# Layer 0's maxima turned two units ahead, lead maxima in written order, and the products of layer 1's modulation dealt anew over three stages

## The chip, the cores and the metric

The kernel runs on one core of a Trainium2 chip. The metric is the device time of one execution in microseconds (us). The engines are TensorE (PE; PEld is its weight load), VectorE (DVE), ScalarE (ACT), GpSimd (POOL) and SyncE (SP), which issues most of the DMAs; ScalarE issues a few as well (ACTq).

## The reference, cut to what matters

Two layers over 1024 latent tokens and 256 context tokens, width 1024, all in 32-bit floats. Layer 0 is grouped-query attention (16 heads, 4 groups of keys and values, head size 64), layer 1 is latent attention (16 heads, keys and values from a compressed 256 columns, queries from 384). Context tokens see only context; latent tokens see both.

```python
def hybrid_layer(x, ctx, c, c_ctx, w_mod, b_mod, norm_w, mixer, mixer_params, cos, sin, with_ctx_out):
    shift, scale, gate = adaln_params(c, w_mod, b_mod)
    shift_c, scale_c, gate_c = adaln_params(c_ctx, w_mod, b_mod)
    h = rms_norm(x, norm_w) * (1.0 + scale[:, None, :]) + shift[:, None, :]
    hc = rms_norm(ctx, norm_w) * (1.0 + scale_c) + shift_c
    y, yc = mixer(h, hc, mixer_params, cos, sin, with_ctx_out)
    x = x + gate[:, None, :] * y
    if with_ctx_out:
        ctx = ctx + gate_c * yc
    return x, ctx
```

`adaln_params` is silu(cond) times a 1024 x 3072 matrix, cut into shift, scale and gate (sections 0, 1 and 2 below). Layer 1 needs shift and scale for both conditions, but its gate only for the latent tokens, at the very end. A mixer projects, normalises queries and keys, rotates them, does softmax attention, multiplies by a silu gate and projects back.

## The kernel before, in words

Every product of 32-bit numbers is made of three products of halves (`mm3`, L105 to L111: high x high, low x high, high x low), with the halves from a cast (L102, L173) and a subtraction (L103, L152). Weights come in pieces of 512 KB through a pool of three buffers, `rawp`, tag `wraw` (`load_weight`, L154): DMA on SP (L169), cast on ACT (L173), subtraction on DVE or POOL (L152). The stages, by the time of the profile:

- Up to about 260 us, a planner (`Plan.at(step, function)`, L276) lays out the projections of layer 0: keys and values, queries, and the first gate tiles. Each tile ends on DVE with L103 to L123 lines; L1123 makes the `t` that TensorE transposes at L1131.
- To 359 us, the rest of the gates of layer 0, in slices of 512 columns by m steps (`gate_slice`, L331; per group c, g an index m from 0 to 3): eight times three products per slice into `mm`, ACT and DVE (L343) behind them. In between, the first two attention units are started (`start_unit`: SP loads KA, KB, QA, QL), and their maxima are computed (the lead).
- To 726 us, attention of layer 0 in 20 units. A unit is a pair of heads with all its queries: 16 latent units, each 10 key tiles, and 4 context units (numbers 4, 9, 18, 19), each two. Score maxima of a later unit (L475, two products side by side on halves of the array, `mx`; reduced on DVE at L484) run between the scores of the present one.
- To 853 us the output projection, to 958 the keys stage of layer 1 (below), to 1100 its queries, to 1140 its gates, to 1560 its attention, then the last projection.

**Turns.** Before a unit's scores, its maxima must lie as rows. `do_shift` (L499) puts a reduction into one of four tiles and leaves a function in `self.turns`: four transposes of 32 x 32 on DVE (L95) into 32 rows of `turned`, and two DMAs of 4 KB on ACT's queue (L510, `shift<-turned`). `run_turns` (L742) runs them between a unit's scores and its product with the values, for the units up to `next_turn` (L760), the next one with any context units right behind it. Each score gets its shift by a product `st<-shift,minus` at L589 over all rows of `shift`. The last latent unit (number 17) is cut into 6 and 4 key tiles, and runs its turns after the 6. `add_up` sums on POOL (L636), `finish` normalises there too (L733), and SP loads and stores around it (L728, L734 and on).

**Modulation of layer 1.** `mod_cols` (L251) makes one block of 128 rows: DVE multiplies 128 x 1024 weights (`wcols`) with a row of the condition and sums along it (L254), once per condition. Section 0 is done in eight blocks of two products by the planner (L1342 and on), sections 1 (two products a block) and 2 (one) by `some_cols` (L1484) in the gate slices. `mod_cols_end` turns the sums and, for section 2, stores them.

**The keys stage.** For each of ten token tiles: `kv_compress` (PE `mm`, 128x288, norm on ACT, DVE L1650 to L1656 and POOL), `kv_latent` (transposes, split), `kv_expand` (products `mmk`, `mmv`; ACT squares, DVE sums `kss` L1704, POOL roots `kn_rs` L135, DVE scales L1687; ACT copies and SP stores v), and `kv_store` (transposes L1723, cast on ACT L1727, subtraction on DVE L1728, four stores on SP). `staged` (L115) overlaps them: a tile is stored one round after it is expanded. DVE keeps the written order there. Then follow the query projections (`proj1`, 128x384) with `wqa`, the four pieces of `l1_w_in` 128x2x384, the first of them ahead of the last tile's store.

## Time and profile before

| | before |
|---|---|
| median of 3 runs (lowest to highest), us | 1649.63 (1649.48 to 1652.47) |
| profiled execution, us | 1649.71 |
| its span, us | 1647.9 |
| granted clock, mean over the span | 0.992 |
| TensorE busy, us | 1603.8 |
| DVE busy, us | 1142.0 |
| POOL busy, us | 957.7 |
| ACT busy, us | 642.2 |

The span is the time between the first and the last instruction that the profile shows. A row of the timeline has the start, the length, the engine, the line, the operation, the tiles out<-in, and in brackets the engine's idle time before it with what ended it. "x2" joins equal neighbours.

### The profile page before, as it was taken

Reading aid. Unit: us, or ns where it says so; the run is one execution under the profiler, and the core shown is the slowest. Engines: PE = TensorE matmul, PEld = TensorE weight load, DVE = VectorE, ACT = ScalarE, POOL = GpSimd, SP = SyncE. Lnnn points to the kernel's source line nnn. Section 1 sums busy time; section 2 is a strip of 40 time slices with the busy share of each in tenths; the row PEclk is TensorE's granted clock in tenths of the full one; section 3 lists DMA queues with packets and bytes.
Section 4 is the critical chain, followed back from the end, with each engine's and each line's share of the span. In section 5 each row is a group of like instructions: output and inputs, shape, how many; then the busy total and the mean of one; then the engine's idle time right before and its main releaser. Section 6 shows DMA issues by size and latency. Waiting matters only on the chain.

```text
span 1647.9 us, 26555 instructions
## 1 busy us (share of the span) xinstructions
PE 1603.8 (97%) x9836; PEld 1181.2 (72%) x9836; DVE 1142.0 (69%) x1939; ACT 642.2 (39%) x943; POOL 957.7 (58%) x628
## 2 busy tenths in 40 slices
PE   8999899999999999989999999999999999999998
PEld 5776788775555555557887899887766767767587
DVE  3765986678898888716566667765788788788231
ACT  4643221125554655422234543341534444435310
POOL 2773540118899899933334555450768778777521
PEclk9999999999999999999999999999999999999999
DMA  9545667851444332257324776777566565563451
GB/s 320 178 137 180 186 186 234 247 144 46 107 96 107 97 98 78 59 145 223 119 77 131 214 234 174 221 204 196 127 150 143 136 136 121 136 144 76 124 182 66
DMA packets 215358, 246.26 MB, mean 149 GB/s; under 512 B 19962, under 2 KB 157426, under 8 KB 215228
## 3 DMA queue, kind: packets, MB, share of 16 engines
q1 hardware_dynamic: 214260, 244.31, 53.3%
q8 instruction: 78, 1.28, 0.3%
q14 instruction: 52, 0.43, 0.1%
q10 hardware_dynamic: 968, 0.25, 0.1%
HBM read 170.71 MB, written 73.63 MB: 148 GB/s over the span
## 4 chain that ended last, share of the span: by engine, by line
PE 81%; DVE 6%; DMA 5%; POOL 4%; issue 2%; ACT 1%; SPq 1%; ACTq 0%; DVEq 0%; POOLq 0%
PE st L589 19%; PE av L650 8%; PE mm L109 7%; PE avt L650 7%; PE mm L110 7%; PE mm L111 7%; PE mx L441 4%; PE y L109 3%; PE y L111 3%; PE y L110 3%; PE mx L475 2%; DVE wb L152 1%; POOL acp L636 1%; PE mx L451 1%; DVE t L1123 1%
## 5 line engine op out<-in xcount | busy, mean ns | idle before, releaser
L636 POOL TENSOR_TENSOR acp<-acp,p 128x1024 f32<-128x1024 f32 x188 | 448.8, 2387 | 12.6
L596 ACT ACTIVATE p<-st 128x1024 f32<-128x1024 f32 x328 | 336.4, 1027 | 165.0 <-PE st L589 156.4
L443 DVE TENSOR_REDUCE m<-mx 128x1 f32<-128x512 f32 x256 | 175.6, 691 | 65.3 <-PE mx L441 59.4
L636 POOL TENSOR_TENSOR acp<-p 128x1024 f32<-128x1024 f32 x34 | 81.5, 2398 | 201.3 <-ACT p L596 201.2
L484 DVE TENSOR_REDUCE m<-mx 128x1 f32<-128x1024 f32 x128 | 150.8, 1220 | 45.6 <-PE mx L475 44.7
L650 PE MATMUL avt<-p,v 128*64 128x512 f32 x672 | 149.4, 596 | 0.0
L650 PE MATMUL av<-p,v 128*64 128x512 f32 x640 | 141.1, 595 | 0.0
L152 POOL TENSOR_TENSOR wb<-wraw,wa 128x512 fp32r<-128x512 f32 (+3 forms) x65 | 91.1, 1415 | 77.3 <-ACT wa L173 77.2
L109 PE MATMUL mm<-wa,hh 128*128 128x512 f32 (+2 forms) x336 | 125.5, 373 | 2.0 <-ACT hh L1023 2.0
L589 PE MATMUL st<-QH,KH 64*128 64x512 f32 x320 | 122.7, 407 | 0.1
L111 PE MATMUL mm<-wa,hl 128*128 128x512 f32 (+2 forms) x336 | 120.9, 360 | 1.4 <-DVE hl L1026 1.4
L110 PE MATMUL mm<-wb,hh 128*128 128x512 f32 (+2 forms) x336 | 120.6, 359 | 0.0
L589 PE MATMUL st<-QH,KL 64*128 64x512 f32 x320 | 118.1, 391 | 0.0
L589 PE MATMUL st<-QL,KH 64*128 64x512 f32 x320 | 117.7, 390 | 0.0
L109 PE MATMUL y<-wa,oh 128*128 128x512 f32 (+1 forms) x296 | 114.1, 386 | 2.0 <-DVE yt L880 1.4
L111 PE MATMUL y<-wa,ol 128*128 128x512 f32 (+1 forms) x296 | 113.5, 384 | 0.6 <-DVE ol L863 0.6
L110 PE MATMUL y<-wb,oh 128*128 128x512 f32 (+1 forms) x296 | 113.5, 383 | 0.0
L650 PEld LDWEIGHTS avt<-p,v 128*64 128x64 f32 x672 | 46.3, 137 | 93.2 <-issue 85.0
L650 PEld LDWEIGHTS av<-p,v 128*64 128x64 f32 x640 | 44.4, 137 | 87.9 <-issue 87.3
L109 PE MATMUL mm<-hh,wa 128*128 128x512 f32 (+1 forms) x264 | 104.0, 394 | 0.0
L110 PE MATMUL mm<-hl,wa 128*128 128x512 f32 (+1 forms) x264 | 102.5, 388 | 0.0
L111 PE MATMUL mm<-hh,wb 128*128 128x512 f32 (+1 forms) x264 | 102.1, 387 | 0.0
(259 smaller groups left out, 4026.7 us busy)
## 6 DMA issues: line engine op xcount, KB each, us to landing
wraw<-in_l_w_in SPq DMA_DIRECT2D x28, 512.0 KB
wcols<-in_l_w_mod_t SPq DMA_DIRECT2D x24, 512.0 KB
KH<-k1h SPq DMA_DIRECT2D x32, 320.0 KB
KL<-k1l SPq DMA_DIRECT2D x32, 320.0 KB
rb<-rrow SPq DMA_DIRECT2D x72, 128.0 KB
mraw<-in_l_w_mod SPq DMA_DIRECT2D x16, 512.0 KB
wraw<-in_l_w_out SPq DMA_DIRECT2D x16, 512.0 KB
QA<-q0h SPq DMA_DIRECT2D x32, 256.0 KB
```

Source lines behind the costliest of these rows:

```text
L109: pe.matmul(ps, lhsT=lh(k), rhs=rh(k), start=first and i == 0, stop=False)
L110: pe.matmul(ps, lhsT=lh(k), rhs=rl(k), start=False, stop=False)
L111: pe.matmul(ps, lhsT=ll(k), rhs=rh(k), start=False, stop=last and i == len(ks) - 1)
L152: eng.tensor_sub(lo, a, b)
L441: pe.matmul(held["m"][:, cs], lhsT=q[:, t * P:(t + 1) * P], rhs=k[:, ks], start=j == 0, stop=j == len(pairs) - 1)
L443: dve.reduce_max(s["m"][:, i, n:n + 1], held["m"], axis=AX.X)
L475: pe.matmul(m[:, n * 512:n * 512 + 512], lhsT=q[:, i * P:(i + 1) * P], rhs=k[:, n * 512:n * 512 + 512], start=True, stop=True)
L484: dve.reduce_max(s["m"][:, i, 0:1], m, axis=AX.X)
L589: pe.matmul(ps[:, n * 512:(n + 1) * 512], lhsT=lh, rhs=rh, start=j == 0, stop=j == last)
L596: act.activation(p, ps, AF.Exp, scale=self.ops["scale"])
L636: pool.tensor_add(t, a, b)
L650: pe.matmul(s["av"][64 * n:64 * n + 64, :], lhsT=s["v"][:, kt, u["vc"]:u["vc"] + 64], rhs=p[:, n * 512:(n + 1) * 512], start=kt == kts[0], ...
```

## The change

- **Turns.** `next_turn` now also goes over context units that follow the next unit, so a context unit is turned two units ahead of itself, and `turned` has three places (rows 0, 32 and 96) by turns.
- **Lead.** The gate slices of group 1 from (m = 0, column 512) on are written out in fixed order on TensorE, and two pairs of maxima at a time stand behind slices (1, 1024) to (3, 512), with one group of them in the middle of (3, 0). Both lead units are started together.
- **Loads of a new group of keys.** KA, then QA and QL, then KB.
- **Modulation.** Section 0: five blocks by the planner, ten single products at steps 107.2 to 133 where eight pairs stood at steps 82.2 to 131.2. The gate slices get the three blocks left of section 0 and section 1 (22 products for 24). Section 2 goes to the keys stage of layer 1: one product behind `kv_store` of tiles 0 to 7, from weights in `rawp` (tag `wraw`), written in place.

Where rows move. On TensorE in the lead, before (mm are gate products, mx the maxima of a lead unit):

```order
L111 MATMUL mm_3178<-hh_130,wb_2371 128x512
L475 MATMUL mx_3046<-KA_2960,QA_2966 128x512 x2
L109 MATMUL mm_3178<-hh_130,wa_2370 128x512
L110 MATMUL mm_3178<-hl_131,wa_2370 128x512
L111 MATMUL mm_3178<-hh_130,wb_2371 128x512
L475 MATMUL mx_3079<-KA_2960,QA_2966 128x512 x2
```

After:

```order
L109 MATMUL mm_3050<-hhc_748,wa_2352 128x256
L110 MATMUL mm_3050<-hlc_749,wa_2352 128x256
L111 MATMUL mm_3050<-hhc_748,wb_2353 128x256
L475 MATMUL mx_3079<-KA_2897,QA_2901 128x512 x2
L475 MATMUL mx_3083<-KA_2897,QA_2901 128x512 x2
L109 MATMUL mm_3087<-hh_130,wa_2352 128x512
```

Behind three gate products stood one pair of maxima, and so on; now two pairs of maxima stand together behind a whole slice.

On ScalarE near the end of layer 0's attention, before (p are the exponentials of unit 16's last tile and unit 17's first six, the DMAs its turns):

```order
L596 ACTIVATE p_6627<-st_6784 128x1024
L510 DMA shift_2954<-turned_89 1x4x128 x2
L671 COPY os_6840<-avt_6801 128x512
L596 ACTIVATE p_6844<-st_6853 128x1024
L596 ACTIVATE p_6844<-st_6863 128x1024
L596 ACTIVATE p_6845<-st_6875 128x1024
L596 ACTIVATE p_6845<-st_6886 128x1024
L596 ACTIVATE p_6846<-st_6899 128x1024
L596 ACTIVATE p_6846<-st_6910 128x1024
L510 DMA shift_2954<-turned_89 1x4x128 x4
L596 ACTIVATE p_6956<-st_6960 128x1024
```

After:

```order
L596 ACTIVATE p_6602<-st_6759 128x1024
L510 DMA shift_2891<-turned_89 1x4x128 x6
L671 COPY os_6827<-avt_6776 128x512
L596 ACTIVATE p_6831<-st_6840 128x1024
L596 ACTIVATE p_6831<-st_6850 128x1024
L596 ACTIVATE p_6832<-st_6862 128x1024
L596 ACTIVATE p_6832<-st_6873 128x1024
L596 ACTIVATE p_6833<-st_6886 128x1024
L596 ACTIVATE p_6833<-st_6897 128x1024
L596 ACTIVATE p_6931<-st_6935 128x1024
```

The four copies for the units 18 and 19 moved from behind unit 17's first six tiles to the turn of unit 16, where two stood.

On DVE at the end of the keys stage, before (from tile 7's store on; kss to kn belong to tile 9):

```order
L1728 SCALAR_TENSOR_TENSOR tl_9427<-tp_9421,w_kn_7173,th_9426 128x512
L1728 SCALAR_TENSOR_TENSOR tl_9438<-tp_9432,w_kn_7173,th_9437 128x512
L1704 TENSOR_REDUCE kss_9459<-sq_9457 128x8
L133 TENSOR_SCALAR kn_ms_9461<-kss_9459 128x8
L1704 TENSOR_REDUCE kss_9485<-sq_9483 128x8
L133 TENSOR_SCALAR kn_ms_9487<-kss_9485 128x8
L1687 TENSOR_TENSOR kn_9468<-mmk_9443,kn_rs_9463 128x512
L1687 TENSOR_TENSOR kn_9495<-mmk_9469,kn_rs_9489 128x512
L1728 SCALAR_TENSOR_TENSOR tl_9503<-tp_9497,w_kn_7173,th_9502 128x512
L1728 SCALAR_TENSOR_TENSOR tl_9514<-tp_9508,w_kn_7173,th_9513 128x512
```

After:

```order
L1737 SCALAR_TENSOR_TENSOR tl_9439<-tp_9433,w_kn_7148,th_9438 128x512
L254 SCALAR_TENSOR_TENSOR wcols_9444,cols2_71<-wcols_9444,u0_8249 128x1024
L152 TENSOR_TENSOR wb_9531<-wraw_9538,wa_9530 128x384
L260 TENSOR_TENSOR top3_84<-cols2_71,colsT_112 128x8
L95 STREAM_TRANSPOSE turned_89<-top3_84 32x32 x4
L1713 TENSOR_REDUCE kss_9469<-sq_9467 128x8
L152 TENSOR_TENSOR wb_9531<-wraw_9544,wa_9530 128x384
L133 TENSOR_SCALAR kn_ms_9471<-kss_9469 128x8
L1713 TENSOR_REDUCE kss_9495<-sq_9493 128x8
L133 TENSOR_SCALAR kn_ms_9497<-kss_9495 128x8
L1696 TENSOR_TENSOR kn_9478<-mmk_9453,kn_rs_9473 128x512
L1696 TENSOR_TENSOR kn_9505<-mmk_9479,kn_rs_9499 128x512
```

Between the store and the next tile's sums stand the modulation product of block 7, its end, and two halves of the query weights' subtractions (L152), which before stood some tiles ahead. (Lines after the first edits count higher in the changed kernel: its L1737 is L1728 of before.)

The diff:

```diff
--- before.py
+++ after.py
@@ -248,9 +248,9 @@
                 dve.tensor_tensor(s1, tv, bias, op=ALU.add)
                 dve.scalar_tensor_tensor(A[l][:, ks, :], s1, 1.0, nw, op0=ALU.add, op1=ALU.mult)
 
-    def mod_cols(w, u, junk, sec, k, conds=2):
-
-        for j in range(conds):
+    def mod_cols(w, u, junk, sec, k, conds):
+
+        for j in conds:
             dve.scalar_tensor_tensor(junk, w, 0.5, u[:, j, :], op0=ALU.mult, op1=ALU.mult, accum_out=sums_of[sec][:, k, j:j + 1])
 
     def mod_cols_end(sec):
@@ -503,7 +503,7 @@
             dve.reduce_max(m[:, :8], s["m"], axis=AX.X)
 
             def turn():
-                at_ = 32 * (self.units.index(u) % 2)
+                at_ = (0, 32, 96)[self.units.index(u) % 3]
                 r = turned[at_:at_ + 32, :]
                 turn_squares(r, raw(m))
                 for n in range(2):
@@ -759,6 +759,8 @@
                     cut = 6 if u is self.last_lat else 0
                     next_turn = t + 1
                     while next_turn + 1 < len(self.units) and len(self.units[next_turn]["kts"]) <= 4:
+                        next_turn += 1
+                    while next_turn + 1 < len(self.units) and len(self.units[next_turn + 1]["kts"]) <= 4:
                         next_turn += 1
                     if not WIDE[self.l]:
                         next_turn = None
@@ -1339,8 +1341,8 @@
         sp.dma_start(w, ins["l1_w_mod_t"][sec * D + k * P:sec * D + (k + 1) * P, :])
         gate_in[k] = w
 
-    def cols_mult(sec, k):
-        mod_cols(gate_in.pop(k), gate_in["u"], small.tile([P, D], BF16, name="junk", tag="junk", bufs=1), sec, k)
+    def cols_mult(sec, k, j):
+        mod_cols(gate_in[k], gate_in["u"], small.tile([P, D], BF16, name="junk", tag="junk", bufs=1), sec, k, (j,))
 
     plan.at(46, more_room)
     at_step = 47.6
@@ -1356,10 +1358,10 @@
     plan.at(67.8, cols_room)
     for j in range(2):
         plan.at(72.5 + 4 * j, cond_rows, j)
-    for k in range(KT):
-        plan.at(77 + 7 * k, cols_fetch, 0, k)
-        plan.at(82.2 + 7 * k, cols_mult, 0, k)
-    plan.at(138, mod_cols_end, 0)
+    for k, steps in enumerate(((107.2, 111.2), (115.2, 119.2), (121.5, 124), (126.5, 128.5), (131, 133))):
+        plan.at(steps[0] - 6, cols_fetch, 0, k)
+        for j in range(2):
+            plan.at(steps[j], cols_mult, 0, k, j)
     weight("g1", 2048, 120, (120.2, 122.2, 124.2, 127.2), (125.2, 127.1, 129.2, 132.2))
     for m in range(2):
         for s0 in range(0, NT, 512):
@@ -1409,22 +1411,27 @@
         g = u["g"]
         r = slice(64 * (g % 2), 64 * (g % 2) + 64)
         lat = u["kind"] == "lat"
+        new = False
         if g not in at.kcache:
             KA = kp.tile([P, NT], F32R, name="KA", tag="KA")
             KB = kp.tile([P if HALVES[0] else 65, NT], F32R, name="KB", tag="KB")
             if HALVES[0]:
-                for t, src in ((KA, k0h), (KB, k0l)):
-                    for n in range(2):
-                        sp.dma_start(raw(t[64 * n:64 * n + 64, :]), src[g // 2, r, :])
+                for n in range(2):
+                    sp.dma_start(raw(KA[64 * n:64 * n + 64, :]), k0h[g // 2, r, :])
             else:
                 sp.dma_start(raw(KA[0:64, :]), k0h[g // 2, r, :])
                 sp.dma_start(raw(KA[64:128, :]), k0l[g // 2, r, :])
                 sp.dma_start(raw(KB[0:64, :]), k0h[g // 2, r, :])
                 pool.memset(raw(KB[64:65, :]), -1.0)
+            new = True
             at.kcache[g] = dict(KA=KA, KB=KB)
         KA, KB = at.kcache[g]["KA"], at.kcache[g]["KB"]
         if HALVES[0]:
-            return l0_load_halves(u, at, lat, KA, KB)
+            s = l0_load_halves(u, at, lat, KA, KB)
+            if new:
+                for n in range(2):
+                    sp.dma_start(raw(KB[64 * n:64 * n + 64, :]), k0l[g // 2, r, :])
+            return s
         qp = at.qp if at.started % 4 < 3 else at.qp2
         QA = qp.tile([P, NL], F32R, name="QA", tag="QA")
         QB = qp.tile([65, NL], F32R, name="QB", tag="QB")
@@ -1479,15 +1486,15 @@
     for j in range(2):
         sp.dma_start(u[:, j, :], ud[j:j + 1, :].broadcast_to([P, D]))
     junk = mw.tile([P, D], BF16, name="junk", tag="junk", bufs=1)
-    blocks = [(sec, k) for sec in (1, 2) for k in range(KT)]
+    blocks = [(0, k) for k in range(5, KT)] + [(1, k) for k in range(KT)]
 
     def some_cols(n):
 
-        for _ in range(n):
+        for _ in range(min(n, len(blocks))):
             sec, k = blocks.pop(0)
             w = mw.tile([P, D], F32, name="wcols", tag="wcols")
             sp.dma_start(w, ins["l1_w_mod_t"][sec * D + k * P:sec * D + (k + 1) * P, :])
-            mod_cols(w, u, junk, sec, k, 3 - sec)
+            mod_cols(w, u, junk, sec, k, range(2))
             if k == KT - 1:
                 mod_cols_end(sec)
 
@@ -1499,20 +1506,22 @@
     pieces = []
     wo = [load_weight(ins["l0_w_out"], KT, 0, 512, 2, todo=pieces)]
     with tc.tile_pool(name="wkg0b", bufs=2, **right) as wkg:
-        for s0 in (0, 512):
-            gate_slice(0, 1, 0, s0, 512, ws["g1"], hT, ps_mm, wkg)
-            some_cols(2)
-            at.step += 1
-        pieces.pop(0)()()
+        gate_slice(0, 1, 0, 0, 512, ws["g1"], hT, ps_mm, wkg)
+        at.step += 1
     stG.close()
     at.open_early(stE)
-    at.start_unit()
-    with tc.tile_pool(name="wkg0b", bufs=2, **right) as wkg:
+    for _ in range(2):
+        at.start_unit()
+
+    def two_maxima():
+        at.maxima(at.done + 2, 2)
+
+    with tc.tile_pool(name="wkg0b", bufs=2, **right) as wkg, tc.manual_schedule(engines={mybir.EngineType.PE}):
         for m in range(4):
-            for s0 in range(0, NT, 512) if m else (1024,):
-                gate_slice(0, 1, m, s0, min(512, NT - s0), ws["g1"], hT, ps_mm, wkg)
-                if (m, s0) != (3, 1024):
-                    at.maxima(min(at.done + 2, 14), 2)
+            for s0 in range(0, NT, 512) if m else (512, 1024):
+                gate_slice(0, 1, m, s0, min(512, NT - s0), ws["g1"], hT, ps_mm, wkg, {KT // 2: two_maxima} if (m, s0) == (3, 0) else {})
+                if (m, s0) >= (1, 1024) and (m, s0) != (3, 1024):
+                    two_maxima()
                 at.step += 1
                 at.run_turns()
                 if s0 == 512:
@@ -1731,8 +1740,20 @@
 
         kept = []
 
+        u = st.enter_context(tc.tile_pool(name="urow1", bufs=1, **right)).tile([P, D], F32, name="u0", tag="u0")
+        sp.dma_start(u, ud[0:1, :].broadcast_to([P, D]))
+
+        def gate_cols(k):
+            w = rawp.tile([P, D], F32, name="wcols", tag="wraw")
+            sp.dma_start(w, ins["l1_w_mod_t"][2 * D + k * P:2 * D + (k + 1) * P, :])
+            mod_cols(w, u.unsqueeze(1), w, 2, k, (0,))
+            if k == KT - 1:
+                mod_cols_end(2)
+
         def store_all_but_last(tt, held):
             kept.append(held) if tt == TT - 1 else kv_store(tt, held)
+            if tt < KT:
+                gate_cols(tt)
 
         with in_order(mybir.EngineType.DVE):
             staged(range(TT), kv_compress, kv_latent, later, later, kv_expand, store_all_but_last)
```

## The prediction

> **What bounds the kernel now.** I read the page first, then the windows for the granted clock, then the waits of TensorE in the timeline, and last the rows of the engines that end those waits. Two lines of the page:
>
> ```profile
> span 1647.9 us, 26555 instructions
> PE 1603.8 (97%) x9836; PEld 1181.2 (72%) x9836; DVE 1142.0 (69%) x1939; ACT 642.2 (39%) x943; POOL 957.7 (58%) x628
> ```
>
> TensorE is busy for 1603.8 of 1647.9 us. The number of its products isn't changed, so this change can win only at the 44 us in which it idles, at the time in which it runs at half clock, and at pairs of products that follow each other badly. The windows show the clock (columns: window, length, busy time of PE, PEld, DVE, ACT, POOL, then the granted clock, the DMA share and GB/s):
>
> ```profile
> 200.00:210.00 10.00, 7.75 (x33) 6.49 (x33) 9.66 (x13) 2.22 (x4) 6.15 (x4) 0.83 0.58 176
> 320.00:330.00 10.00, 8.10 (x21) 4.99 (x21) 2.02 (x2) 0.98 (x2) 0.00 (x0) 0.66 1.04 249
> 530.00:540.00 10.00, 7.55 (x34) 3.68 (x32) 4.64 (x3) 2.11 (x3) 7.35 (x4) 0.83 0.51 129
> 700.00:720.00 20.00, 14.86 (x104) 8.33 (x102) 3.00 (x4) 6.51 (x7) 8.78 (x6) 0.83 0.50 136
> ```
>
> A clock of 0.83 over 10 us is 3.4 us at half clock, of which half, 1.7 us, is lost; 0.66 over 10 us and 0.83 over 20 us are 6.8 us, 3.4 lost. Each of these windows holds one wait of TensorE (start, length, instruction, in brackets the idle time before it and what ended it):
>
> ```profile
> 187.64 0.66 PE L1131 MATMUL tp<-ident,t 128*128 128x128 f32 x4 [1.83 <-DVE t L1123]
> 202.25 1.08 PE L1131 MATMUL tp<-ident,t 128*128 128x128 f32 x4 [2.29 <-DVE t L1123]
> 321.90 1.19 PE L475 MATMUL mx<-KA,QA 64*128 64x512 f32 x2 [2.83 <-issue]
> 536.56 0.76 PE L589 MATMUL st<-shift,minus 64*128 64x512 f32 x1 [2.16 <-DMA shift<-turned]
> 706.89 0.79 PE L589 MATMUL st<-shift,minus 64*128 64x512 f32 x1 [5.14 <-DMA shift<-turned]
> ```
>
> So a wait of 2.16 to 5.14 us is followed by 3.4 or 6.8 us at half clock, and the one of 1.83 is not. The change touches the causes of all five waits. [...]
>
> **Projections.** DVE has eight pairs of modulation products in this stage, ahead of L1123, whose result TensorE's transposes wait for:
>
> ```profile
> 181.85 1.22 DVE L254 SCALAR_TENSOR_TENSOR junk<-wcols,urow 128x1024 bf16<-128x1024 f32 x1
> ...
> 183.11 2.19 DVE L254 SCALAR_TENSOR_TENSOR junk<-wcols,urow 128x1024 bf16<-128x1024 f32 x1
> ...
> 185.23 1.75 DVE L152 TENSOR_TENSOR wb<-wraw,wa 128x512 fp32r<-128x512 f32 x1
> ...
> 194.87 1.22 DVE L254 SCALAR_TENSOR_TENSOR junk<-wcols,urow 128x1024 bf16<-128x1024 f32 x1
> ```
>
> The pair at 181.85 takes 1.22 + 2.19 = 3.4 us of the chain before the wait of 1.83; the pair that ends with 194.87 takes 2.4 before the wait of 2.29. Both pairs leave these places: more goes than was waited for, so both waits go, with the clock after the second: 1.83 + 2.29 + 1.7 = 5.8. Ten single products come back, in later tiles and each behind L1123. There one delays the next tile's chain by 1.22, and the L152 of 1.75 still stands in the chain of the four tiles that load gate weights; I leave 0.8 for what stays. Taken: **-5.0**, bounds -3.0 and -5.8.
>
> **Gate slices.** DVE does 22 products here instead of 24 and TensorE waits nowhere between 288 and 319 us, so nothing is to be had; the cover is TensorE's own products. What counts is that DVE's last one comes earlier, because the loads of the lead units start behind it.
>
> **Lead.** First the ends of the m steps of group 1's gates (m = 1, 2, and the end of m = 3), with two of the maxima between them, then the loads on SP, and of DVE's products the one that is the last in the new order (two follow it now):
>
> ```profile
> 302.38 0.40 PE L109 MATMUL mm<-hh,wa 128*128 128x512 f32 x1
> ...
> 316.15 0.40 PE L109 MATMUL mm<-hh,wa 128*128 128x512 f32 x1
> ...
> 329.87 0.50 PE L475 MATMUL mx<-KA,QA 64*128 64x512 f32 x2
> ...
> 331.19 0.49 PE L475 MATMUL mx<-KA,QA 64*128 64x512 f32 x2
> ...
> 359.08 0.50 PE L475 MATMUL mx<-KA,QA 64*128 64x512 f32 x2
> ```
>
> ```profile
> 312.17 1.16 SPq L1418 DMA_DIRECT2D KA<-k0h  x2
> ...
> 315.93 0.60 SPq L1395 DMA_DIRECT2D QA<-q0h  x1
> ```
>
> ```profile
> 305.82 1.23 DVE L254 SCALAR_TENSOR_TENSOR junk<-wcols,urow 128x1024 bf16<-128x1024 f32 x1
> ```
>
> A bare m step takes 316.15 - 302.38 = 13.77 us, for 60 products of 512 columns (0.23 each). Steps 2 and 3 take 359.08 - 316.15 = 42.93, that is 15.4 more than two bare ones: 2.83 of wait, 3.4 of half clock, and 9.2 for 14 pairs of maxima. A pair itself takes 0.23 (3.2 in all), and the period 329.87 to 331.19, three products and one pair, is 1.32 instead of 4 x 0.23 = 0.91: 0.4 us for going over from one kind to the other and back, 14 times, the other 5.9. After the change the same pairs stand in seven groups: 7 x 0.4 = 2.9, so 3.0 go. The loads start when DVE's last product has left their room, and now begin with KA, go on with QA, and leave KB to the last. The product at 305.82 ends at 307.1, so KA is issued between 307.1 and 308.5 (a small store that stood ahead of it is gone) and no longer at 312.17. From KA's issue to the first maxima took 321.90 - 312.17 = 9.7; the two KB loads that stood in between (655 KB at the 249 GB/s of that window) are 2.6 of it. That gives 314.2 to 315.6, ahead of 316.15, where the first maxima now stand. So wait and half clock go as well: 2.83 + 3.4 + 3.0 = 9.2, taken as **-9.0** for small waits on the two score buffers; bounds -6.5 (2 us of wait, half a window of low clock less) and -9.8.
>
> **Turns.** The copies of the turned maxima into the shift rows, issued on ScalarE's queue (length from first issue to last), and first products behind a turn:
>
> ```profile
> 504.05 4.55 ACTq L510 DMA_DIRECT2D shift<-turned  x2
> 525.10 7.53 ACTq L510 DMA_DIRECT2D shift<-turned  x4
> ...
> 681.39 1.23 ACTq L510 DMA_DIRECT2D shift<-turned  x2
> 695.43 9.09 ACTq L510 DMA_DIRECT2D shift<-turned  x4
> ```
>
> ```profile
> 511.98 0.40 PE L589 MATMUL st<-QA,KA 64*128 64x512 f32 x2
> ...
> 689.23 0.40 PE L589 MATMUL st<-shift,minus 64*128 64x512 f32 x2
> ```
>
> At the end of the stage the four copies of 695.43 are issued by 704.5 and land 2.4 us later, at 706.89: 5.14 of wait and 3.4 of half clock. Now all six belong to the turn of 681.39. At that turn's rate (1.23 for two) they take 3.7, are issued by 685.1 and land 2.4 to 3.9 later, by 689.0; the first product that reads them ran at 689.23 without a wait. So **-8.5**, bounds -8.5 and +2.3 (at the rate of the 7.53 row six take 11.3, land at 696.6, and 7.4 of wait and 3.4 of clock come back).
>
> At unit 9's start 2.16 + 1.7 = 3.9 go, since two copies remain there and not four. But the four now stand one unit earlier, at 504.05, where the queue was slow too. In the 7.53 row the last copy, held back on a semaphore that a load of SP used before it, landed 3.9 after the last issue. Moved there, four are issued between 509.8 (4.55 + 1.2) and 511.6 (7.53) and land by 511.8 to 515.5, against products that read them from 512.7 on: 0 to 2.8 of wait, up to 1.7 of clock. Taken: **-2.5**, bounds -3.9 and +0.6.
>
> **Keys.** Eight products move to the keys stage of layer 1, with nine loads of 512 KB through the three slots that the next weights use. The rows: a wait of DVE in a long tile and the splits of two short ones, the key transposes of two short tiles and the query projection on TensorE, and what a piece of weights takes from issue over cast to split:
>
> ```profile
> 896.17 0.69 DVE L1704 TENSOR_REDUCE kss<-sq 128x8 f32<-128x512 f32 x1 [1.12 <-ACT sq L1702]
> ...
> 944.60 1.40 DVE L1728 SCALAR_TENSOR_TENSOR tl<-tp,w_kn,th 128x512 fp32r<-128x512 f32 x2
> ...
> 950.82 1.40 DVE L1728 SCALAR_TENSOR_TENSOR tl<-tp,w_kn,th 128x512 fp32r<-128x512 f32 x2
> ```
>
> ```profile
> 946.33 1.03 PE L1723 MATMUL tp<-ident,kn 128*128 128x128 f32 x8
> ...
> 952.67 1.03 PE L1723 MATMUL tp<-ident,kn 128*128 128x128 f32 x8
> 953.46 0.42 PE L109 MATMUL mm<-wa,hh 128*128 128x384 f32 x1
> ...
> 957.73 1.03 PE L1723 MATMUL tp<-ident,kn 128*128 128x128 f32 x8
> ```
>
> ```profile
> 924.84 0.37 SPq L169 DMA_DIRECT2D wraw<-in_l_w_in  x1
> ```
>
> ```profile
> 928.26 0.51 ACT L173 CAST wa<-wraw 128x384 fp32r<-128x384 f32 x1 [1.46 <-DMA wraw<-in_l_w_in]
> ```
>
> ```profile
> 925.98 1.04 POOL L152 TENSOR_TENSOR wb<-wraw,wa 128x384 fp32r<-128x384 f32 x1 [0.33 <-ACT wa L173]
> ```
>
> The first products of the stage stand in long tiles, where one wait of DVE for ScalarE (1.12) already covers nearly all of 1.22; they hide. In the last tiles DVE goes round in 950.82 - 944.60 = 6.22 us against TensorE's 952.67 - 946.33 = 6.34: a product of 1.22 there makes DVE the slower one, and what covers it is only that the splits of the query weights (the row of 925.98 is one) leave the tiles before. Three such products come ahead of the split of 950.82, 3.7 us less the slack of about 2.2 that I give DVE for those splits and for 0.1 a tile: it moves to 952.3, and the last product ends at 952.3 + 1.4 + 1.2 = 954.9. Before, the four pieces of the query weights were loaded by 925. Now each takes its slot from a product: the third is issued behind the last product. Loaded and cast as in the rows (928.26 - 924.84 = 3.4) and split (0.5 + 1.04) it is there at 959.8; TensorE wants it in the middle of 953.46 to 957.73. The fourth is issued behind a store that waits on ScalarE behind the third's cast, about 959.8, is cast from 963.2, and half of it is split by DVE behind the next tile's L1728, by about 965.7. TensorE wants it at 956.7: 9.0 late, the third's wait within it. Two waits of over 2.16 give at least one stretch at half clock, 1.7. Taken: **+10.7**; bounds +4 (no lag on DVE, pieces landing in 2 us) and +15 (6.8 us more at half clock, and slower loads).
>
> **How the numbers follow.** -5.0 - 9.0 - 8.5 - 2.5 + 10.7 = -14.3. The profiled execution took 1649.71, the median is 1649.63; 1649.7 - 14.3 = **1635.4 us**. What a measurement here can tell from no change is 0.2%, 3.3 us.
>
> The rivals:
> - **The weights are not late.** If the third and fourth piece come through before 956, the four gains stand alone: 1649.7 - 25.0 = 1624.7. For it: a piece needs only 3.4 us from issue to cast. Against: the slot of the third is held until the last product. 0.16.
> - **DVE becomes the bound of the keys stage, and the kernel is slower.** If none of the eight products is hidden and each is stretched as in the row of 183.11, they cost 8 x 2.19 = 17.5; with 9.0 and 3.4 for the late weights 29.9, so 1649.7 - 25.0 + 29.9 = 1654.6. It decides from 28.3 us in this stage on. Against: in the long tiles DVE has waits that take a product in. 0.06.
> - **The lead doesn't get its loads earlier.** If KA and QA come 3 us later than I put them, 2.83 and 3.4 stay: 1641.6. For it: the margin above is 0.5 to 2 us; against: what holds their issue back, DVE's products, is cut. 0.14.
> - **The wait moves with the copies.** If six copies go at the slow rate, 10.8 comes back at unit 17: 1646.2. For it: 9.09 for four; against: 1.23 for two at that very turn. 0.10.
> [...]
>
> The forecast keeps 0.50; its own bounds are about 1629 to 1642. The range 1624 to 1646 takes in the first, third and last rival and nearly all of the fourth. Faster by over 0.2%: 0.88; within: 0.05; slower: 0.07 (the second rival and a little of the fourth with late weights).
>
> **What would show it.** In the profile after: no waits of over 1 us at L1131 between 180 and 225; the gate steps m = 2 and 3 in about 34 us without a low clock; no wait near 703, perhaps one of 1 to 3 us near 512; and a wait of TensorE of 7 to 10 us in two parts at the first 128x384 products of layer 1, with a low clock there. The prediction is wrong if that last wait is missing or twice as long, or if copies at 681 take over 8 us.

## The result, and the profile after

| | before | after |
|---|---|---|
| median, us (runs beside each other) | 1649.48 (7) | 1638.80 (7) |
| lowest to highest, us | 1645.92 to 1653.03 | 1636.82 to 1642.93 |
| profiled execution, us | 1649.71 | 1642.93 |
| granted clock, mean over the span | 0.992 | 0.996 |

The ratio is 0.9937, with a 95% interval of 0.9923 to 0.9951, that is 10.4 us less (8.1 to 12.7). The execution that was profiled after the change happens to be the longest of its seven, so its trace shows only 6.8 of it. From its page, the busy time of each engine:

```profile
PE 1599.2 (97%) x9836; PEld 1185.3 (72%) x9836; DVE 1143.3 (70%) x1939; ACT 640.8 (39%) x943; POOL 958.7 (58%) x628
```

The number of products is the same. I cut both traces at the same instructions of TensorE (their starts in the timelines) and compare stage by stage:

| from, to | before | after | change | predicted |
|---|---|---|---|---|
| start to the transposes of the fifth tile, 78.00 / 81.82 | 78.00 | 81.82 | +3.8 | 0 |
| to the first gate product of group 1, 288.60 / 285.92 | 210.60 | 204.10 | -6.5 | -5.0 |
| to the first scores, 359.42 / 347.64 (the lead) | 70.82 | 61.72 | -9.1 | -9.0 |
| to the scores behind the waits of units 8 and 9, 564.63 / 548.79 | 205.21 | 201.15 | -4.1 | -2.5 |
| to the output projection, 727.68 / 705.13 | 163.05 | 156.34 | -6.7 | -8.5 |
| to the first key transposes of layer 1, 886.78 / 867.05 | 159.10 | 161.92 | +2.8 | 0 |
| to the last transposes of `qan` of the first queries, 1007.11 / 999.46 | 120.33 | 132.41 | +12.1 | +10.7 |
| to the last product, 1643.18 / 1636.36 | 636.07 | 636.90 | +0.8 | 0 |

The five stages that the change touches give -14.3 together, as forecast; the three that it doesn't touch give +7.4. Two of these vary from run to run by themselves: the same transposes began at 78.98 and 79.14 in the profiles of the first and the ninth experiment below, in which nothing before it differs from the changed kernel; and the wait for `yt` at the head of the output projection, 1.43 in the trace of before and 3.74 in that of after, was between 1.11 and 3.75 in the eleven experiments, near 1.1 to 1.7 in seven of them and 2.6 to 3.8 in four. So most of this belongs to the run and not to the change. Not all of the start can be settled: in the one profile of before the transposes of the fifth tile began at 78.00, ahead of all twelve profiles of the changed kernel and the experiments (78.59 to 81.93). The stages that the change touches repeat better. Over the profiles of experiments that leave them alone, the projections took 204.03 to 204.15, the lead 61.72 to 61.73 and the keys stage 132.21 to 132.94; the attention of layer 0 took 356.80 to 357.49, but 358.79 in the sixth experiment and 360.15 in the tenth.

**Clock.** The windows of after that answer to those of before:

```profile
200.00:210.00 10.00, 10.00 (x48) 7.98 (x48) 9.93 (x15) 3.41 (x6) 7.14 (x6) 1.00 0.35 108
320.00:330.00 10.00, 10.00 (x57) 7.90 (x57) 6.93 (x8) 2.18 (x4) 0.00 (x0) 1.00 0.73 204
530.00:540.00 10.00, 10.00 (x92) 7.06 (x90) 9.89 (x13) 8.22 (x8) 9.69 (x6) 1.00 0.73 169
700.00:720.00 20.00, 19.43 (x113) 13.72 (x110) 4.43 (x6) 4.08 (x5) 7.14 (x5) 1.00 0.57 161
940.00:945.00 5.00, 0.90 (x4) 0.30 (x2) 3.04 (x7) 0.45 (x2) 3.24 (x2) 0.79 0.77 219
945.00:950.00 5.00, 4.81 (x17) 4.21 (x18) 2.19 (x5) 1.25 (x4) 1.00 (x1) 0.53 0.73 195
```

All four low windows of before are at 1.00; a new one stands at 940 to 950, in the keys stage. One more, 0.66 over 730 to 735, lies behind the wait for `yt` of 3.74, in a stage that the change leaves alone.

**TensorE's waits**, at the places of the five of before, and then in the keys stage:

```profile
189.49 0.60 PE L1133 MATMUL tp<-ident,t 128*128 128x128 f32 x4
...
201.48 0.63 PE L1133 MATMUL tp<-ident,t 128*128 128x128 f32 x4
...
313.57 0.73 PE L475 MATMUL mx<-KA,QA 64*128 64x512 f32 x4
...
501.19 0.47 PE L589 MATMUL st<-shift,minus 64*128 64x512 f32 x1 [0.97 <-DMA shift<-turned]
...
685.57 0.40 PE L589 MATMUL st<-shift,minus 64*128 64x512 f32 x2
...
933.00 0.50 PE L109 MATMUL mmk<-wa,kvh 128*128 128x512 f32 x1 [1.06 <-DVE kn L1696]
...
941.05 0.44 PE L110 MATMUL mm<-wb,hh 128*128 128x384 f32 x1 [0.76 <-DVE wb L152]
...
945.11 1.01 PE L109 MATMUL mm<-wa,hh 128*128 128x384 f32 x2 [3.45 <-ACT wa L173]
...
960.65 0.52 PE L1882 MATMUL tp<-ident,qan 128*128 128x128 f32 x3 [1.23 <-DVE qan L1875]
```

The two at the transposes, the one at the first maxima and the one of the last unit are gone, the one of 2.16 has become one of 0.97 a unit earlier. What came is 0.49, 0.44 and 1.06 for `kn` in three short tiles, 0.76 and 3.45 for weights, and 1.23 for `qan`.

**The lead and the turns**, on SP's and ScalarE's queues, and the DVE product that ends last before the loads:

```profile
304.38 1.15 SPq L1420 DMA_DIRECT2D KA<-k0h  x2
...
306.86 0.60 SPq L1397 DMA_DIRECT2D QA<-q0h  x1
```

```profile
303.12 1.23 DVE L254 SCALAR_TENSOR_TENSOR junk<-wcols,urow 128x1024 bf16<-128x1024 f32 x1
```

```profile
491.54 6.47 ACTq L510 DMA_DIRECT2D shift<-turned  x4
...
665.60 3.91 ACTq L510 DMA_DIRECT2D shift<-turned  x6
```

The product ends at 304.35 and KA is issued at 304.38. The six copies at 665.60 took 3.91 (I had put 3.7), the four at 491.54 took 6.47.

### The profile page after: what moved, and what is told of

It reads as the page before. It is cut to its first block, busy times and chain, and to the rows that moved or that the text cites. A ratio compares the mean times of both kernels' runs of the same rounds, so it can differ in the third digit from the quotient of the medians.

```text
span 1641.1 us, 26569 instructions
## 1 busy us (share of the span) xinstructions
PE 1599.2 (97%) x9836; PEld 1185.3 (72%) x9836; DVE 1143.3 (70%) x1939; ACT 640.8 (39%) x943; POOL 958.7 (58%) x628
## 4 chain that ended last, share of the span: by engine, by line
PE 82%; DMA 5%; POOL 4%; DVE 4%; issue 3%; ACT 1%; SPq 1%; ACTq 0%; DVEq 0%; POOLq 0%
PE st L589 20%; PE av L650 9%; PE mm L109 8%; PE avt L650 8%; PE mm L111 8%; PE mm L110 7%; PE mx L441 4%; PE y L109 4%; PE y L110 4%; PE y L111 4%; PE mx L475 2%; DVE wb L152 1%; PE mx L451 1%; PE tp L1133 1%; PE pm L216 1%
## 5 line engine op out<-in xcount | busy, mean ns | idle before, releaser
L152 POOL TENSOR_TENSOR wb<-wraw,wa 128x512 fp32r<-128x512 f32 (+3 forms) x65 | 91.9, 1427 | 78.1 <-ACT wa L173 78.1
```

Of the source, the lines that this page charges most:

```text
L152: eng.tensor_sub(lo, a, b)
```

## The experiments

Each is one edit of the changed kernel. Time differences are taken from ratios to before, measured beside it. An interval is some 0.15 to 0.2% on either side, 3 us, so where less matters I go by the traces, cut as in the table.

**1. Turns undone.** Context units are turned one unit ahead again, with two places.

```diff
-                at_ = (0, 32, 96)[self.units.index(u) % 3]
+                at_ = 32 * (self.units.index(u) % 2)
...
-                    while next_turn + 1 < len(self.units) and len(self.units[next_turn + 1]["kts"]) <= 4:
-                        next_turn += 1
```

> The changed kernel with the turns as before (each context unit turned by the unit right ahead of its neighbours, two places in turned). The traces put 4.1 us at units 8 and 9 and 6.7 us at unit 17 on the turns. Theory: part of that is given back at once in the output projection, where TensorE now waits 3.74 us for yt (1.43 before) since the last units' stores are not earlier; with the old turns that wait falls back to about 1.5, and the kernel is some 8 us slower than the changed one. Rival: the longer wait in the output projection has nothing to do with the turns; it stays at 3.7 and the kernel is some 10.8 us slower. Second rival: the six copies at one turn cost something too, and the kernel is less than 6 us slower.

1646.32 us, ratio 0.9976 (0.9965 to 0.9988): 6.4 us more than the changed kernel. From the first scores to the output projection it took 366.85, against 357.49 changed and 368.26 before. The four copies stand behind the six tiles again, and so does the wait:

```profile
678.62 9.05 ACTq L510 DMA_DIRECT2D shift<-turned  x4
```

```profile
689.91 0.79 PE L589 MATMUL st<-shift,minus 64*128 64x512 f32 x1 [4.97 <-DMA shift<-turned]
```

The four take 9.05, as in before (9.09), so the length goes with four copies at that place. In the trace the turns are worth 9.4 of the 10.8 that attention gained. The wait for `yt` was short here, 1.11; but it is as short in experiments that keep the turns (1.31 in the second), so the gain isn't given back there, and that theory falls. The times alone don't separate the 6.4 from the theory's 8 or from the second rival's 6: the two intervals are about 2 us on either side.

**2. Narrow products in the keys stage.** Each of the eight products takes 32 of its 1024 columns and leaves out the rest of its sum; the loads stay.

```diff
-            mod_cols(w, u.unsqueeze(1), w, 2, k, (0,))
+            mod_cols(w[:, :32], u[:, :32].unsqueeze(1), w[:, :32], 2, k, (0,))
```

> The changed kernel with the eight products of the keys stage cut to 32 of their 1024 columns (the sums of section 2 leave out the rest); loads, slots, the end of the section and its store stay. Theory: the length of the products on DVE makes DVE the slower engine in the short tiles (3.2 us by the trace) and pushes the last product, the end of the section and with it the fourth piece's load back; about 5 us faster than the changed kernel, with a wait of about 1 to 3 us left for the fourth piece. Rival: the late weights are set by slots and queues alone; only the 3.2 go. Second rival: the products are the whole cost; 12 us faster, no wait left at the first 128x384 products.

1633.34 us, ratio 0.9901 (0.9883 to 0.992): 6 us less than the changed kernel. The keys stage took 127.96, 7.6 above before and 4.5 below the changed kernel. TensorE's two longest waits up to the last `qan` now:

```profile
929.38 0.45 PE L109 MATMUL mm<-wa,hh 128*128 128x384 f32 x1 [1.84 <-ACT v L1718]
...
947.34 0.52 PE L1882 MATMUL tp<-ident,qan 128*128 128x128 f32 x3 [1.62 <-DVE qan L1875]
```

The waits for `kn` in the short tiles are gone with the multiplication. But 7.6 of the 12.1 stay though DVE multiplies next to nothing: the larger part of the price doesn't come from the products' length. What remains in this run are the loads in the three slots and the section's end. By the trace the weights are in it: ScalarE waits 4.42 for a piece (its cast is at 927.01), and the copy of `v` behind that cast is what the wait of 1.84 is for. No run takes the loads away and keeps the products, so the share of each is not shown.

**3. Products early.** Two products a tile in tiles 0 to 3, none after.

```diff
-            if tt < KT:
-                gate_cols(tt)
+            if tt < KT // 2:
+                gate_cols(2 * tt)
+                gate_cols(2 * tt + 1)
```

> The changed kernel with two products a tile behind the stores of tiles 0 to 3, none behind 4 to 7. Theory: the products in the short tiles and the late slots are the cost, and the long tiles have room for most of two products (DVE waits 0.56 and 1.12 us for ScalarE in them, against 2.44): no wait for query weights, no DVE wait in the short tiles, 9 to 12 us faster than the changed kernel. Rival: the nine loads and the DMA traffic are the cost wherever they stand; within 3 us of the changed kernel.

1635.98 us, ratio 0.991 (0.9893 to 0.9927): 4.4 less, not the 9 to 12 expected. The query weights are in time, but the long tiles take one product and not two:

```profile
908.86 0.47 PE L109 MATMUL mmv<-wa,kvh 128*128 128x512 f32 x1 [3.54 <-DVE kvn L1665]
```

The second product of a tile is late by 0.85 at 884.23 and by 0.84 at 895.20, and behind the last, where TensorE waits 3.54, comes the section's end as well.

**4. The section's end late.** `mod_cols_end(2)` (a sum, four transposes, the store `gated<-turned`) moves behind the last tile's store.

```diff
-            if k == KT - 1:
-                mod_cols_end(2)
...
             kv_store(TT - 1, kept[0])
+            mod_cols_end(2)
```

> The changed kernel with the end of section 2 (its addition, four transposes on DVE and its small store on SP) put behind the last tile's store, out of the way of the query weights. Theory: the small store stands ahead of the fourth piece's load on SP and holds it about 3 us (939.84 against the last product's end at 937.5); without it the piece is issued 2 to 3 us earlier and the kernel is 2 to 4 us faster than the changed one. Rival: the slot that the last product holds, or the store of v ahead of the load, sets the issue; no difference beyond 1 us.

1638.58 us, ratio 0.9926 (0.9909 to 0.9944): 1.8 less, within the noise. The trace tells more. In the changed kernel SP's queue read:

```profile
929.69 1.55 SPq L169 DMA_DIRECT2D wraw<-in_l_w_in  x2
...
939.84 0.29 SPq L263 DMA_DIRECT2D gated<-turned  x1
940.23 0.37 SPq L1719 DMA_DIRECT2D vd<-v  x1
940.65 0.45 SPq L169 DMA_DIRECT2D wraw<-in_l_w_in  x1
```

With the store out of the way the fourth piece follows a store of v at 931.57, 2.9 earlier when both are counted from the first tile's key transposes, and the wait for it is 2.34 in place of 3.45:

```profile
936.89 0.44 PE L109 MATMUL mm<-wa,hh 128*128 128x384 f32 x1 [2.34 <-ACT wa L173]
```

Between the last two key transposes that is 2.3 less, and 1.5 of it is lost again by the last `qan`. So the store does hold the fourth piece back, and mending that alone is worth little.

**5. Section 2 in the attention of layer 1.** The eight products move out of the keys stage, one to a unit, with the row of the condition in a slot of `rawp`.

```diff
+                        if end and self.l == 1:
+                            if cols:
+                                cols()
+                            cols = more.pop(0)() if more else None
...
+            held_u["u"] = rawp.tile([P, D], F32, name="u0", tag="wraw")
...
+    more = [lambda: None] * 5 + [lambda k=k: gate_cols(k) for k in range(KT)]
+    at.run(24, 2, pieces, lambda: first.extend(fetch_first(1, 3)), more)
```

> The changed kernel with the eight products of section 2 taken out of the keys stage and put into layer 1's attention, one behind the turn of each of units 6 to 13, its weights loaded a unit ahead through the same three slots (the condition's row holds one of them). Theory: the keys stage is as before again (12 us less by the trace), and DVE has room in a unit of 25.3 us in which it is busy for 20.3, so the kernel is 8 to 12 us faster than the changed one, with TensorE without waits in layer 1's attention. Rival: next to POOL the products take 2.2 and delay the maxima that TensorE waits for, 1 to 2 us a unit, and nothing or less than 3 us is won.

1633.9 us, ratio 0.9898 (0.9878 to 0.9917): 6.4 less than the changed kernel, where 8 to 12 were expected. The keys stage is back at 120.33, its length before to the hundredth: all 12.1 are the products and their loads. But behind the queries the trace has 6.7 more than the changed kernel's, nearly all in one unit (31.4 us where its neighbours take 25.4). There SP waits for a slot, since the row holds one of the three, and the loads of the next unit stand behind the waiting one. TensorE then waits for QH, 0.68 at 1346.09 and 0.97 at 1348.67:

```profile
1337.55 0.36 SPq L2000 DMA_DIRECT2D wcols<-in_l_w_mod_t  x1
...
1338.45 0.47 SPq L1780 DMA_DIRECT2D KH<-k1h  x1
```

```profile
1348.67 0.76 PE L441 MATMUL mx<-KH,QH 64*128 64x512 f32 x1 [0.97 <-DMA QH<-q1h]
```

**6. The projections' products in pairs again.** The same ten products, but two at a time in every other tile.

```diff
-    for k, steps in enumerate(((107.2, 111.2), (115.2, 119.2), (121.5, 124), (126.5, 128.5), (131, 133))):
-        plan.at(steps[0] - 6, cols_fetch, 0, k)
+    for k in range(5):
+        plan.at(77 + 7 * k, cols_fetch, 0, k)
         for j in range(2):
-            plan.at(steps[j], cols_mult, 0, k, j)
+            plan.at(82.2 + 7 * k, cols_mult, 0, k, j)
```

> The changed kernel with the same ten products of section 0 in the projections, but as five pairs at the old steps (82.2 and every 7 steps), ahead of L1123 again. Theory: their place is what cost; the waits of 1.83 and 2.29 and the low clock behind the second come back, and the kernel is 4 to 6.5 us slower than the changed one. Rival: fewer products are what helped (ten for sixteen); within 2 us of the changed kernel, no wait over 1 us.

1647.86 us, ratio 0.9986 (0.9972 to 1.0): 8 more than the changed kernel, 6.7 of it in this stage by the trace.

```profile
191.61 0.66 PE L1133 MATMUL tp<-ident,t 128*128 128x128 f32 x4 [1.83 <-DVE t L1125]
...
206.21 0.63 PE L1133 MATMUL tp<-ident,t 128*128 128x128 f32 x4 [2.29 <-DVE t L1125]
```

The waits of before (1.83, 2.29, and one of 0.35 at 221.99, here at 226.17) are back to the hundredth with ten products where before had sixteen. So between sixteen and ten it is the place that counts and not the number. The rest of the 8 is in the attention of layer 0, 1.3 longer in this trace, with waits of 0.96 and 1.64 at the turn of four copies; the edit doesn't touch that.

**7. The lead without the written order.**

```diff
-    with tc.tile_pool(name="wkg0b", bufs=2, **right) as wkg, tc.manual_schedule(engines={mybir.EngineType.PE}):
+    with tc.tile_pool(name="wkg0b", bufs=2, **right) as wkg:
```

> The changed kernel without the written order on TensorE in the gate slices of group 1, so that the scheduler lays the maxima between the products again; loads and modulation stay as changed. Theory: the wait for KA and QA stays away, but the going over between products and maxima comes back, some seven more times at 0.4: about 3 us slower than the changed kernel. Rival: the order is worth nothing, the loads were all; within 1 us. Second rival: the scheduler puts the first maxima ahead of their loads again, 6 to 9 us slower.

1639.88 us, ratio 0.9933 (0.9915 to 0.995): the same time. Left to itself the scheduler laid the maxima in nearly the same groups (310.84 x4, 317.21 x4, 323.54 x4, and so on). The lead takes 62.16 for 61.72. The written order is worth nothing that these runs can tell; the grouping comes, it seems, from where the maxima are called.

**8. KB first.** In a new group of keys KB is loaded right behind KA again.

```diff
-                for n in range(2):
-                    sp.dma_start(raw(KA[64 * n:64 * n + 64, :]), k0h[g // 2, r, :])
+                for t, src in ((KA, k0h), (KB, k0l)):
+                    for n in range(2):
+                        sp.dma_start(raw(t[64 * n:64 * n + 64, :]), src[g // 2, r, :])
...
-            if new:
-                for n in range(2):
-                    sp.dma_start(raw(KB[64 * n:64 * n + 64, :]), k0l[g // 2, r, :])
```

> The changed kernel with KB loaded ahead of QA and QL again. Theory: the second QA is then issued 1.2 us later than at 306.86, and by the 6 us from that issue to the first maxima before, it is there at about 314.0 against first maxima at 313.6: at most a wait of 1 us, no low clock, no difference that can be measured. Rival: the 655 KB ahead delay QA by 2.6 us or more, and TensorE waits 2 us or more with 1.5 to 3 us of low clock: 3 to 5 us slower.

1639.44 us, ratio 0.9946 (0.9926 to 0.9967). The first maxima wait 1.16 for QA at 312.96, no low clock follows, and from the projections' fifth tile to the first scores the trace has 1.8 more. So by the trace the order of the loads is worth 1 to 2 us of the lead's 9.

**9. Experiment 5 with the row in a room of its own**, one unit later.

```diff
+    held_u = {"u": stE.enter_context(tc.tile_pool(name="urow1", bufs=1, **right)).tile([P, D], F32, name="u0", tag="u0")}
...
+    more = [lambda: None] * 6 + [lambda k=k: gate_cols(k) for k in range(KT)]
```

> As the run with section 2's products in layer 1's attention, but with a tile of its own for the condition's row, so that all three weight slots stay free, and a unit later. There one unit took 31.4 us in place of 25.4 (two waits for QH, whose loads stood on SP behind a load that waited for a slot, and a low clock); all other units were as before. Theory: that one unit was the whole price, and with the slots free it goes: some 6 us faster than that run, 11 to 13 us faster than the changed kernel, all units at 25.2 to 25.6. Rival: other loads of weights still stand ahead of QH or KH for a slot; one unit of over 28 us stays and 3 us or less is won against that run.

**1628.57 us**, ratio 0.9866 (0.9845 to 0.9886): 22 us under before and some 12 under the changed kernel by the ratios, 10 by the medians. Both intervals lie apart, so this version beats both kernels. The keys stage takes 120.34, and attention has none of the waits of experiment 5, though two of the products there take 3.24 and 3.22. From the last `qan` to the last product it took 637.13, within what the traces have without section 2 there (634.70 to 637.70).

**10. Five products in the keys stage, three in the projections** as singles.

```diff
+    for k, (load, step) in enumerate(((92, 99.2), (96, 103.2), (129.5, 136))):
+        plan.at(load, cols_fetch, 2, k)
+        plan.at(step, cols_mult, 2, k, 0)
...
-            if tt < KT:
-                gate_cols(tt)
+            if tt < KT - 3:
+                gate_cols(tt + 3)
```

> The changed kernel with five of section 2's products in the keys stage, behind the stores of tiles 0 to 4 (the long tiles), and three in the projections as singles behind L1123 (steps 99.2, 103.2 and 136). Theory: in the long tiles one product a tile is hidden, the slots are free before the query weights are wanted, and three singles behind L1123 cost nothing: all of the keys stage's 12 us come back, 9 to 12 us faster than the changed kernel. Rival: the weights are still late because the store of section 2's end and the casts come with the last long tile; 5 us or less is won. Second rival: three more singles bring waits of over 1 us back at L1131.

1634.09 us, ratio 0.9909 (0.9889 to 0.993): some 4.6 less, half of what was expected. The keys stage took 124.68, 7.7 less than changed but 4.4 more than before: the split of a piece of weights and the section's end now stand on DVE behind the last product (912.90 to 915.67), ScalarE waits 2.17 for the next subtraction there, and its copy of `v` stands behind that wait:

```profile
916.94 0.50 PE L109 MATMUL mmv<-wa,kvh 128*128 128x512 f32 x1 [1.74 <-ACT v L1721]
920.08 0.50 PE L109 MATMUL mmk<-wa,kvh 128*128 128x512 f32 x1 [1.48 <-DVE kn L1699]
```

In the projections one of the three cost a wait of 1.05. And the attention of layer 0, which the edit leaves alone, took 2.7 more in this trace: its turn of four copies took 8.39, TensorE waited 1.44 and 1.03 for them, and the clock was 0.66 over 500 to 505.

**11. A block of section 0 computed a second time** in the gate slices, so that DVE has 24 products ahead of the lead's loads again.

```diff
-    blocks = [(0, k) for k in range(5, KT)] + [(1, k) for k in range(KT)]
+    blocks = [(0, k) for k in range(4, KT)] + [(1, k) for k in range(KT)]
```

> The changed kernel with block 4 of section 0 computed a second time in the gate slices, so that DVE has 24 products there again and not 22. If the lead's loads wait for DVE's last product, that product ends 2.45 us later than at 304.27, KA is issued at about 306.8 (304.38 in the changed kernel), the second QA load at about 309.3, and the first maxima, which stand at 313.6, get a wait of 0.5 to 2.5 us back: +0.5 to +4 with the clock. The rival: the loads came earlier because KA and QA now stand ahead of KB, or because a small store ahead of them is gone, and the number of products has no part in it: KA is issued by 305, no wait, within 0.5 us.

1642.26 us, ratio 0.9957 (0.9942 to 0.9972): 3.3 more. From the projections' fifth tile to the first scores the trace has 3.8 more, and the chain from DVE over SP to TensorE can be read off:

```profile
304.54 1.23 DVE L254 SCALAR_TENSOR_TENSOR junk<-wcols,urow 128x1024 bf16<-128x1024 f32 x1
```

```profile
305.80 1.16 SPq L1420 DMA_DIRECT2D KA<-k0h  x2
...
308.44 0.58 SPq L1397 DMA_DIRECT2D QA<-q0h  x1
```

```profile
314.44 1.01 PE L475 MATMUL mx<-KA,QA 64*128 64x512 f32 x3 [1.30 <-DMA QA<-q0h]
```

KA goes out as the product ends (305.77), 6.9 before the first maxima at 312.68; in the changed kernel it goes out 9.2 before them. The waits are 0.44 and 1.30, with a clock of 0.69 over 315 to 320. So two products hold the loads back, by 2.8 against the maxima (without the wait of 0.44 KA would stand 6.4 ahead). The same count stood in before, yet KA went out only 4.0 ahead of the slice's end there (312.17 against 316.15). So of the 5.2 that the loads won, some 2.4 has another cause. In before the end of section 2 stood behind the last product on DVE, and its store right ahead of KA on SP:

```profile
311.82 0.29 SPq L263 DMA_DIRECT2D gated<-turned  x1
```

DVE also waited 0.93 for the last of the products' weights there. No run takes these apart.

## Why the prediction held, step by step

The forecast was 1635.4 and the range 1624 to 1646; 1638.8 lies in it, 3.4 above the forecast. The direction and the places of gain and loss hold. That the touched stages sum to the forecast -14.3 to the tenth is luck: the terms are off by -1.5, -0.1, +1.8, -1.6 and +1.4, in the order below, and cancel. By the medians the change is worth 10.4, and the interval (8.1 to 12.7) leaves 14.3 out. The 3.9 between the two can't be placed with one profile of before: the stages that the change leaves alone differ between profiles by as much (the start 78.59 to 81.93, the output projection 158.30 to 162.83).

- **Projections: -6.5 for -5.0**, beyond the bound of -5.8. Both waits went with the clock, and also the small one of 0.35 that I hadn't counted; and nothing of the 0.8 stayed that I had left for the single products. From 177.63 on TensorE goes round in 5.9 to 6.0 without a wait. Experiment 6 shows the cause.
- **Lead: -9.1 for -9.0.** The loads are issued behind DVE's last product, at 304.38 (forecast 307.1 to 308.5 in the time of before, where the stage begins 2.7 later), and the first maxima don't wait. Experiment 11 shows that two products more bring 3.8 of it back; experiment 8 gives 1 to 2 to the order of the loads; experiment 7 gives nothing to the written order. What the end of section 2 and the grouping are worth no run shows by itself; for the grouping there is the trace. A slice of 24 products takes 5.71 (314.23 to 319.94) for 5.51 at 0.2295 each, a group of two pairs 0.66 (313.57 to 314.23) for 0.46: 0.4 a group for going over, as put.
- **Turns of the last units: -6.7 for -8.5.** The mechanism is right to the copy: 3.91 for six, and no wait at 685.57. Six copies there took 3.88 to 3.92 in all eleven profiles that have these turns. (By the profile's list of DMAs a copy is 2 KB, not 4.) The size was off in the clock. Of the 6.8 us at half clock I had counted half as lost, 3.4; but its first part lay within the wait of 5.14 itself, as the windows of before show:

```profile
700.00:705.00 5.00, 1.75 (x11) 0.67 (x7) 0.00 (x0) 0.00 (x0) 4.84 (x4) 0.87 0.42 107
705.00:710.00 5.00, 3.11 (x14) 2.65 (x16) 0.00 (x0) 1.60 (x2) 3.91 (x3) 0.50 0.88 234
```

  TensorE was idle until 706.89, so low clock from 706.89 to about 710.5 is all that cost anything: 3.6 at half, 1.8 lost. 5.14 + 1.8 = 6.9.
- **Units 8 and 9: -4.1 for -2.5**, a little beyond the bound of -3.9. The four copies took 6.47, between my two of 5.75 and 7.53, and landed 0.97 late without a low clock: that alone is -2.9. The rest are waits of before that I hadn't counted: 0.30 at 533.93 (the window of 530 to 540 holds two waits, not one) and one for QA, which can't be put down to the turns, since with the turns undone (experiment 1) it was 0.38:

```profile
500.36 0.50 PE L475 MATMUL mx<-KA,QA 64*128 64x512 f32 x1 [1.13 <-DMA QA<-q0h]
```

  Nor is this term firm. In the other profiles with these turns the four copies took 5.89 to 8.39, and the waits for them came to 0.20 to 2.60 together; in the tenth experiment a low clock came back with them. In the chains of before and after the last of the four copies is issued as a load of SP (`sg`) lands, and itself takes 4.37 and 3.63 to land:

```profile
529.13 2.90 DMA sg<-sgd
532.03 0.02 issue
532.05 4.37 DMA shift<-turned
```

```profile
494.78 2.63 DMA sg<-sgd
497.41 0.02 issue
497.43 3.63 DMA shift<-turned
```

  How much of the queue's length at that place comes from this no run shows. (With its own 2.4 from issue to landing the 511.8 there is 512.2, which changes no bound.)
- **Keys: +12.1 for +10.7.** The size came out near, the way there only in part, so that part of the size is luck: the weights' waits and their clock cost 6.8 and not 10.7, and two lengths that I had put at nothing, 2.9 and 2.1, made up for it. The wait that was to be 7 to 10 us in two parts came as 0.76 and 3.45. The step that failed is "the third is issued behind the last product". Pieces two and three went out together at 929.69, ahead of the last product at 935.78; as I read it, the first piece's own slot had come free behind its split, which ended at 930.36. The fourth was the late one, and not behind a store that waits for ScalarE: it stood behind `gated<-turned`, which waits for the section's end on DVE.

```profile
935.78 1.77 DVE L254 SCALAR_TENSOR_TENSOR wcols<-wcols,u 128x1024 f32<-128x1024 f32 x1
...
938.95 0.86 DVE L95 STREAM_TRANSPOSE turned<-top 32x32 f32<-32x32 f32 x4
```

  The other part that failed is the slack. I had set DVE's busy time in a short tile against TensorE's period and let 1.5 us of lateness cost nothing until the weights. But the product stands at the head of a chain that leaves DVE and comes back:

```profile
920.49 1.22 DVE L254 SCALAR_TENSOR_TENSOR wcols<-wcols,u 128x1024 f32<-128x1024 f32 x1
...
921.63 0.68 DVE L1713 TENSOR_REDUCE kss<-sq 128x8 f32<-128x512 f32 x1
...
924.33 0.69 DVE L1696 TENSOR_TENSOR kn<-mmk,kn_rs 128x512 f32<-128x512 f32 x1 [1.02 <-POOL kn_rs L135]
```

  The sums `kss` wait for the product, POOL's roots for the sums, `kn` for the roots, and TensorE for `kn`. While DVE idles 1.02 in that chain its free time helps nobody. The key transposes show the sizes:

```profile
906.74 1.03 PE L1732 MATMUL tp<-ident,kn 128*128 128x128 f32 x8
...
936.09 1.04 PE L1732 MATMUL tp<-ident,kn 128*128 128x128 f32 x8
947.96 1.91 PE L1732 MATMUL tp<-ident,kn 128*128 128x128 f32 x8
```

  The four short tiles took 29.35 for 26.45 before (926.22 to 952.67): +2.9. The last one took 11.87 for 5.06 (952.67 to 957.73): +6.8, the waits of 0.76 and 3.45 and the clock of 0.53 behind them (2.35 lost). From there to the last `qan` it is +2.1: the next weights, `l_w_q_b`, come late as well, which I had not counted. The long tiles took 39.69 for 39.44: there the products hide, as put.

**The rivals.** The weights were not in time (without products and loads in it the stage is 12.1 shorter, experiment 5). DVE did bound the short tiles, but for 2.9 us; the whole stage lost 12.1 and not 29.9. The lead's loads came earlier. The wait didn't move with the copies: 3.91 for six. The chances also held 0.04 for low clock that stays when the waits go (1640.5): all four low windows of before went with their waits, and their counterparts are at 1.00. Which wait brings a low clock the traces don't settle by its length: in before it came with the waits of 2.16, 2.29, 2.83 and 5.14 and not with the one of 1.83, and in experiment 11 it came with waits of 0.44 and 1.30 (0.69 over 315 to 320).

## What to carry to other kernels

Small work for an engine with idle time was free in this case only where it stands behind the work that others wait for and the chain through other engines had room (in the keys stage the long tiles took 39.69 for 39.44 and the short ones 29.35 for 26.45; in the projections pairs ahead of L1123 took 6.7 more than singles behind it, experiment 6): look at what is next on that engine and who waits for that, not at its busy share. What the work loads counts too in slots and queues that the next stage's weights need; the same work in a stage with room, and with the weights' slots left free, cost nothing that the trace shows (experiment 9: 637.13, within the 634.70 to 637.70 of the traces without it). A wait's price here is, as I estimate it, the wait plus half of the low clock that outlasts it (at unit 17 5.14 + 1.8 = 6.9, where the stage gained 6.7); the low clock within the wait is already paid.
